# Branch B of a hybrid encoder block put in a fixed order by a list program, with branch A's norm and merge as fillers in single matmuls

## The chip, the cores and the metric

The kernel runs on one core of a Trainium2 chip. The metric is the device time of one execution in microseconds (us). Of TensorE (PE), VectorE (DVE), ScalarE (ACT), GpSimd (POOL) and SyncE (SP), PE does the matmuls and transposes, DVE and ACT the elementwise work, and POOL, SP and ACT issue transfers (DMA).

## The reference

One encoder block on 1024 tokens of 1024 features, in float32. What matters here is its token-mixing half, of which this is the frame:

```python
a_q, a_k, a_v, b_q, b_kv, i_q, i_k, i_w, gates = jnp.split(u @ w_in[l], offsets, axis=-1)
y_a = _diff_attention(a_q, a_k, a_v, slopes_a, lam, lam_init, a_subln_g[l])      # branch A, 4 heads, RMS norm behind
q_abs = jnp.einsum('bshe,rhe->bshr', b_q, w_uk[l])
o_lat = _sparse_indexed_attention(q_abs, c_kv, i_q, i_k, i_w, slopes_b)           # branch B, 8 heads, top-256 keys
y_b = jnp.einsum('bshr,rhe->bshe', o_lat, w_uv[l]).reshape(b, s, B_WIDTH)
g = jax.nn.sigmoid(gates).reshape(b, s, 2, d)
mixed = g[:, :, 0] * (y_a @ w_a_proj[l]) + g[:, :, 1] * (y_b @ w_b_proj[l])
x = _layer_norm(DEEPNORM_ALPHA * x + gate1 * (mixed @ w_o[l]), ln1_g[l], ln1_b[l])
```

The other half is a mixture of 16 experts; the adaLN factors (`mod`, from the condition and `ada_w`) go into both.

## The kernel before, in words

To keep float32 precision, an operand is split into a high and a low half and a product is three matmuls (`mm3`: low x high, high x low, high x high, lines 142, 145, 146). A split costs ACT a copy (L132) and DVE a subtraction (L128).

In order of time there are: the indexer's scores and top-k; branch A's attention, head by head (`a_attend`); branch B's attention (`b_attend`); the merge of B with the gates (the loop at L1111); w_o (`po`, L1194); the router and experts. `weave` (L75) runs two generators in turn by planned costs: `attentions` (L1044), the leaders, and `fillers` (L1066), which gives projections (`proj`, `pj` in the trace), gates, and at its end A's norm `a_norm` (L998) and the merge of A `merge_a` (L1025). `leads` and `follows` tie a filler's matmul to a leader some places back. Within these ties a scheduler that works while the kernel is built puts the instructions of each engine in order.

A head of B has 8 query rows of 128. `softmax_rows` (L768) computes a row's logits (plg: L774 with the keys' low halves, L775 with the high, L777 adds the mask of the selected keys), their minimum with the bias on DVE (L778) and the exponentials on ACT (L780). `transposed_pairs` (L783) transposes the two rows of a pair (ptr, L793) and splits them (pth on ACT, ptl on DVE), and the tail of `b_attend` multiplies by the values (pyb, L958 and L959) and adds the halves (yo, yb L962). After each second head `b_scale` (L981) multiplies by the reciprocal sums (rr, pbc) and splits (ybh, ybl). Heads' operands bqq, bqh, bql and the values bv are loaded by POOL (`b_load`, L920), one head ahead.

A's norm loads ya (L1014) by SP, spreads the factors (pbc, L1018), scales (L1019) and splits into yah, yal. The merge of A takes 8 chunks of w_ab, loaded by ACT's queue and split, and for each chunk and half 12 matmuls into pab (L1036), gates them on DVE (L1038) and stores to gates_d. Its matmuls come three at a time. The merge of B does the same with ybh and adds A's part; beside it the chunks of w_o are scaled by the adaLN gate row (L207) and split (woh, wol). `mod_rows` (L686) sums the adaLN weights adaw on DVE (macc, L694) between the projections.

Tiles rotate in slots (16 of L, 14 of X, 7 of P, 4 of pt and of sg, 2 of wr, wh, wl and b), PSUM in 8 banks: mm 2, lg 3, tp 2, av 1.

Of the kernel before, what the change touches and what calls it, by code (L numbers as in the profile page):

```python
# [12 lines left out]
FT = mybir.dt.float32  # L13
# [73 lines left out]
def block_kernel(ctx: ExitStack, tc, a, out):  # L87
# [680 lines left out]
    def softmax_rows(q, hh, ll, bias, L, sel=None):  # L768

        P = s4("P", "P")  # L770
        mx = tiny("mx")
        for n_, (c0, n) in enumerate(pieces(L)):
            p = bank("plg", "lg")
            leads(PE.matmul(p[:, :n], q, ll[:, c0:c0 + n], start=True, stop=False))  # L774
            PE.matmul(p[:, :n], q, hh[:, c0:c0 + n], start=False, stop=sel is None)  # L775
            if sel is not None:
                PE.matmul(p[:, :n], ident_bf, sel[:, c0:c0 + n], start=False, stop=True)  # L777
            V.tensor_tensor_reduce(P[:, c0:c0 + n], p[:, :n], bias[:, c0:c0 + n], 1.0, mx[:, 5:6] if n_ else 3.0e38,  # L778
                                   OP.add, OP.min, mx[:, 0:1] if n_ or L <= 512 else mx[:, 5:6])
        S.activation(P[:, :L], P[:, :L], AF.Exp, bias=mx[:, 0:1], scale=-1.0, accum_out=mx[:, 1:2])  # L780
        return P, mx
# [149 lines left out]
    rden = cp.tile([128, NB, 8], FT, name="rden")  # L931
    ybh, ybl = [None] * 4, [None] * 4

    def b_attend(c, s, yb):
        q, hh, ll = B.pop((c, s))
        v = bvt[c]
        hd = 2 * c + s
        bias = bias_tile(SL_B[hd])

        def rows(qb):  # L940
            L = (qb + 1) * 128
            sel = None
            if qb >= 2:
                j, o = MPACK[qb]
                sel = msk[j][:, o:o + L]
            P, m = softmax_rows(q[:, qb * 128:qb * 128 + 128], hh, ll, bias[:, 896 - 128 * qb:1024], L, sel)
            V.reciprocal(rden[:, qb, hd:hd + 1], m[:, 1:2])
            return P

        def tail(i, Ps):  # L950
            y = bank("pyb", "av", (128, 256))
            last = 2 * i + 1
            for kb, c0, n, th, tl in transposed_pairs(Ps, i):
                if kb % 2 == 0 and kb:
                    yield True
                mean_squares()
                st = v[kb // 4][:, kb % 4, s, :]
                PE.matmul(y[:, c0:c0 + n], st, tl, start=kb == 0, stop=False)  # L958
                PE.matmul(y[:, c0:c0 + n], st, th, start=False, stop=kb == last)  # L959
            tmp = sb.tile([128, 256], FT, name="yo", tag="yo", bufs=2)  # L960
            copy(tmp[s * 64:s * 64 + 64], y[64:128])
            V.tensor_tensor(yb[s * 64:s * 64 + 64, i * 256:i * 256 + 256], y[0:64], tmp[s * 64:s * 64 + 64], op=OP.add)  # L962
            yield True
            if s == 1 and i == 3:
                b_scale(c, yb)

        return pipelined(rows, tail)

    heads = [(c, s) for c in range(4) for s in range(2)]

    def b_main():
        for n, (c, s) in enumerate(heads):
            if s == 0:
                yb = s4("yb", "P")
            if n + 1 < len(heads):
                while heads[n + 1][0] not in have_bq:
                    yield 0.5
                b_load(*heads[n + 1])
            yield from b_attend(c, s, yb)

    def b_scale(c, yb):  # L981
        ybh[c], ybl[c] = s4("ybh", "L", dt=FR), s4("ybl", "L", dt=FR)
        for half in range(2):
            t = slice(half * 512, half * 512 + 512)
            p = bank("pbc", "tp")
            rr = s2("rr", "sg")
            r = rden[:, half * 4:half * 4 + 4, 2 * c:2 * c + 2].unsqueeze(3).to_broadcast([128, 4, 2, 64])
            copy(rr.rearrange("p (j s e) -> p j s e", j=4, s=2), r, V)
            for j in range(4):
                PE.transpose(p[:, j * 128:j * 128 + 128], rr[:, j * 128:j * 128 + 128], ident)  # L990
            V.tensor_tensor(yb[:, t], yb[:, t], p, op=OP.mult)
            copy(ybh[c][:, t], yb[:, t])
            sub(ybl[c][:, t], yb[:, t], ybh[c][:, t])


    yah, yal = [], []

    def a_norm():  # L998
        ms = yams
        while (3, 3) not in done:  # L1000
            yield 0.5
        V.tensor_scalar(ms[:, 1], ms[:, 0], 2.64e36, (1.0 - LAM_INIT) / 64.0, op0=OP.is_lt, op1=OP.mult)
        V.tensor_scalar(ms[:, 0], ms[:, 0], EPS, 1.0 / 4096.0, op0=OP.add, op1=OP.mult)
        S.activation(ms[:, 0], ms[:, 0], AF.Sqrt)
        V.reciprocal(ms[:, 0], ms[:, 0])
        V.tensor_tensor(ms[:, 0], ms[:, 0], ms[:, 1], op=OP.mult)
        for h in range(4):
            oh, ol = s4("yah", "L", dt=FR), s4("yal", "L", dt=FR)
            yah.append(oh)
            yal.append(ol)  # L1010
            for half in range(2):
                t = slice(half * 512, half * 512 + 512)
                y = s2("ya", "sg")
                dma(y, ya_d[h, :, t])  # L1014
                p = bank("pbc", "tp")
                for j in range(4):
                    i = h * 8 + half * 4 + j
                    PE.transpose(p[:, j * 128:j * 128 + 128], ms[:, 0, i:i + 1].to_broadcast([128, 128]), ident)  # L1018
                V.scalar_tensor_tensor(y, y, gsub, p, op0=OP.mult, op1=OP.mult)  # L1019
                copy(oh[:, t], y)  # L1020
                sub(ol[:, t], y, oh[:, t])
                yield 1.5


    def merge_a():  # L1025
        for c in range(KC):
            w = s4("wab", ("wh", "wl")[c % 2], (128, 2, 512), FR)
            wh, wl = halves(a["w_ab"][c, :, 0:512], w[:, 0], w[:, 1], V, S.dma_start)
            for half in range(2):
                t = slice(half * 512, half * 512 + 512)  # L1030
                g = s2("gate", "sg")
                dma(g, gates_d[c, :, t])
                p = bank("pab", "mm")
                for k in range(4):
                    cs = slice(k * 128, k * 128 + 128)
                    mm3(p, wh[:, cs], wl[:, cs], yah[k][:, t], yal[k][:, t], k == 0, k == 3, True)  # L1036
                    yield 2.5
                V.tensor_tensor(g, p, g, op=OP.mult)  # L1038
                dma(gates_d[c, :, t], g)

    started, have_bq = [-1], set()
    TOPK_MORE = 30.0
# [1 line left out]
    def attentions():  # L1044
        LAG[0] = 12
        yield from scores()
        yield from scaled(1.4, topk())
        yield TOPK_MORE

        hold[0] = filled[0]  # L1050
        LAG[0] = 40
        for h in range(4):
            while h not in A:
                yield 0.5
            started[0] = h
# [5 lines left out]
        LAG[0] = 40  # L1061
# [24 lines left out]
    weave(attentions(), fillers())  # L1086
    run(flush())


    def mixed(name):  # L1090
# [772 lines left out]
```

## Time and profile before

| what | value |
|---|---|
| median of 3 runs | 1381.33 us (1376.26 to 1382.92) |
| profiled execution, its own time | 1378.06 us |
| its span, first to last instruction | 1376.3 us |
| mean granted TensorE clock | 0.957 |
| PE busy | 1244.6 us (90%) |
| DVE busy | 952.8 us (69%) |
| ACT busy | 671.6 us (49%) |
| POOL busy | 125.8 us (9%) |
| branch B, first logits to last values | 603.1 to 870.9 us |

Busy time of PE is the union of its matmuls' records; a record is longer than the interval to the next matmul, since they are pipelined, so the interval between starts is what one costs. In brackets behind an instruction stand the idle time before it and what ended it. A granted clock of 1.00 is 2.4 GHz, the slower level 1.2 GHz.

### The profile page before, as it was taken

To read this page: it belongs to the slowest core of one execution; us is meant where nothing else is said; L and a number is where in the kernel's file an instruction comes from. 1 tells how busy PE (TensorE), PEld (TensorE's weight loads), DVE (VectorE), ACT (ScalarE), POOL (GpSimd) and SP (SyncE) were. 2 spreads that over 40 slices of the span, in tenths; PEclk is the share of its full clock that TensorE was granted. 3 is DMA by queue.
4 is the path that set the end of the run, shared out by engine and by line. 5 is a ranking of instruction groups with operands and counts; after the bars stand their busy time and mean duration, and the time that the engine had idled before them with its cause. 6 is when DMAs were issued, how large, how long until landed. Compare 5 with 4: busy or idle time off the path is not lost. (4 is left out here: it accounts for less than half of the span.)

```text
span 1376.3 us, 18450 instructions
## 1 busy us (share of the span) xinstructions
PE 1244.6 (90%) x6184; PEld 976.1 (71%) x6199; DVE 952.8 (69%) x2065; ACT 671.6 (49%) x1193; POOL 125.8 (9%) x154
## 2 busy tenths in 40 slices
PE   7999999999999999998889998899994888999950
PEld 6876778877777777666667776787873767788830
DVE  6547689783457758664676768787887778877736
ACT  4536662213785555444746556434223556555405
POOL 1000000000000001001001100000002233333120
PEclk9999999999999999998999999999996999999975
DMA  9211442113124317564545531665535798989856
GB/s 363 83 44 70 146 176 85 47 67 121 52 83 145 130 55 235 179 190 124 141 138 149 149 103 54 208 220 173 204 121 203 248 317 268 309 289 305 241 88 248
DMA packets 109526, 226.18 MB, mean 164 GB/s; under 512 B 34144, under 2 KB 40688, under 8 KB 109424
## 3 DMA queue, kind: packets, MB, share of 16 engines
q1 hardware_dynamic: 68992, 164.29, 34.0%
q0 software_dynamic: 35824, 52.23, 14.2%
q10 hardware_dynamic: 4608, 8.39, 1.9%
q8 instruction: 53, 0.87, 0.3%
q14 instruction: 49, 0.40, 0.1%
HBM read 170.15 MB, written 54.64 MB: 163 GB/s over the span
## 5 line engine op out<-in xcount | busy, mean ns | idle before, releaser
L142 PE MATMUL pj<-uh,wl 128*128 128x512 f32 x544 | 221.5, 407 | 1.5 <-ACT bkr L132 0.8
L145 PE MATMUL pj<-ul,wh 128*128 128x512 f32 x544 | 217.3, 399 | 0.0
L146 PE MATMUL pj<-uh,wh 128*128 128x512 f32 x544 | 216.8, 399 | 0.0
L128 DVE TENSOR_TENSOR ewl<-raw,ewh 128x1024 fp32r<-128x1024 f32 x102 | 122.6, 1218 | 33.8 <-ACT ewh L132 32.6
L132 ACT ACTIVATE ewh<-raw 128x1024 fp32r<-128x1024 f32 x102 | 105.8, 1057 | 61.7 <-DMA raw<-w_exp 58.5
L142 PEld LDWEIGHTS pj<-uh,wl 128*128 128x128 f32 x544 | 103.1, 189 | 35.2 <-issue 11.1
L146 PEld LDWEIGHTS pj<-uh,wh 128*128 128x128 f32 x544 | 102.9, 189 | 26.3 <-issue 5.6
L145 PEld LDWEIGHTS pj<-ul,wh 128*128 128x128 f32 x544 | 103.2, 190 | 23.8 <-issue 5.1
L132 ACT ACTIVATE pth<-ptr 128x512 fp32r<-128x512 f32 (+1 forms) x120 | 65.7, 551 | 70.2 <-PE ptr L793 38.9
L128 DVE TENSOR_TENSOR ptl<-ptr,pth 128x512 fp32r<-128x512 f32 (+1 forms) x120 | 75.3, 633 | 24.8 <-ACT pth L132 24.3
L142 PE MATMUL pgu<-ewh,xl 128*128 128x512 f32 x200 | 80.7, 404 | 0.9 <-DVE xl L128 0.6
L793 PE MATMUL ptr<-ident,P 128*128 128x128 f32 x432 | 72.5, 284 | 9.4 <-DVE ptl L128 7.9
L146 PE MATMUL pgu<-ewh,xh 128*128 128x512 f32 x200 | 79.0, 395 | 0.0
L145 PE MATMUL pgu<-ewl,xh 128*128 128x512 f32 x200 | 78.9, 394 | 0.0
L765 ACT ACTIVATE P<-P,mx 128x128 f32<-128x128 f32 (+7 forms) x64 | 49.4, 772 | 41.4 <-DVE mx L762 38.1
L793 PEld LDWEIGHTS ptr<-ident,P 128*128 128x128 f32 x432 | 51.9, 146 | 17.6 <-DVE ptl L128 8.2
L1631 POOL DMA_INDIRECT acc_d<-ot,idxs x24 | 46.7, 1946 | 188.4 <-DVE ot L1630 113.7
L128 DVE TENSOR_TENSOR wl<-raw,wh 128x512 fp32r<-128x512 f32 x68 | 44.8, 685 | 23.2 <-ACT wh L132 22.8
L780 ACT ACTIVATE P<-P,mx 128x128 f32<-128x128 f32 (+3 forms) x64 | 49.4, 772 | 22.8 <-DVE mx L778 21.6
L758 PE MATMUL plg<-ak,aq 64*128 64x512 f32 (+4 forms) x288 | 58.2, 375 | 0.9 <-DVE mx L762 0.9
L444 DVE SCALAR_TENSOR_TENSOR sc<-relu,iw,sc 128x512 f32<-128x512 f32 (+3 forms) x70 | 45.4, 654 | 18.2 <-ACT relu L439 16.3
L142 PE MATMUL po<-woh,mxl 128*128 128x512 f32 x128 | 52.5, 410 | 3.2 <-DVE r L1213 3.0
(440 smaller groups left out, 2893.7 us busy)
## 6 DMA issues: line engine op xcount, KB each, us to landing
raw<-w_exp SPq DMA_DIRECT2D x102, 512.0 KB, 8.3
raw<-w_main SPq DMA_DIRECT2D x68, 256.0 KB, 3.2
adaw<-ada_b SPq DMA_DIRECT2D x32, 512.0 KB, 4.7
adaw<-ada_a SPq DMA_DIRECT2D x16, 512.0 KB, 10.1
gates_d<-gt SPq DMA_DIRECT2D x32, 256.0 KB, 2.0
gate<-gates_d SPq DMA_DIRECT2D x32, 256.0 KB, 4.0
xt<-xT SPq DMA_DIRECT2D x8, 512.0 KB, 9.2
bv_d<-bvs SPq DMA_DIRECT2D x16, 256.0 KB, 2.9
```

Source lines behind the costliest of these rows:

```text
L128: e.tensor_tensor(o, i0, i1, op=OP.subtract)
L132: return S.activation(o, i, AF.Copy)
L142: i = PE.matmul(o, wl, xh, start=first, stop=False)
L145: PE.matmul(o, wh, xl, start=False, stop=False)
L146: e = PE.matmul(o, wh, xh, start=False, stop=last)
L444: V.scalar_tensor_tensor(acc, r[:, :n], w, acc, op0=OP.mult, op1=OP.add)
L758: i = PE.matmul(p[:, :n], q[a_][r, qs], k[b_][r, c0:c0 + n], start=m == 0, stop=m == 2)
L765: S.activation(P[:, :L], P[:, :L], AF.Exp, bias=mx_[:, 0:1], scale=-1.0, accum_out=mx_[:, 1:2])
L780: S.activation(P[:, :L], P[:, :L], AF.Exp, bias=mx[:, 0:1], scale=-1.0, accum_out=mx[:, 1:2])
L793: leads(PE.transpose(p[:, c:c + 128], Ps[s][:, kb * 128:kb * 128 + 128], ident))
L1631: G.indirect_dma_start(out=acc_d, out_offset=bass.IndirectOffsetOnAxis(ap=isc, axis=0), in_=ot, in_offset=None, compute_op=OP.add)
```

## The change

`b_attend`, `b_main`, `b_scale`, `a_norm` and `merge_a` give way to `b_stage`. It describes every step of the 8 heads, of A's norm and of A's merge as a node: an engine, a planned duration, a priority, the nodes it depends on, and the slots and banks it takes and gives back. A loop then repeatedly takes the node that can start earliest by this plan (ties by priority: heads by their number, fillers 1000, A's factors and gating -1) and writes its instructions; for PE, DVE and ACT the written order is the order of execution. It runs after the weave, so all projections and A's attention stand ahead of it. The merge of A is 192 nodes of one matmul each. The loads of w_ab go from ACT's queue to SP's, yb from a slot of P to one of wl, rr from sg to wr, and A's pbc from the bank tp to mm.

```diff
+    def b_stage():
+        HOP = 0.35
+        nodes, tokens = [], {"lg": 3, "tp": 2, "av": 1, "mm": 2, "P": 7, "pt": 4, "wl": 2, "wh": 2, "sg": 4, "b": 2, "wr": 2}
...
+                    lg = node("PE", (3 if sel else 2) * 0.00045 * w + 0.05, prio, [lg, prev_row], logits,
+                              take=("lg",) + (("P",) if n_ == 0 else ()))
+                    mins.append(node("DVE", 0.16 + 0.00105 * w, prio, [lg] + mins[-1:], least, give=(("lg", lg),)))
...
+                e = node("ACT", 0.42 + 0.00095 * L, prio, mins, exp)
...
+                    tr = node("PE", 0.00095 * w, prio, [rows_[0][1], rows_[1][1], prev_turn], turn, take=("tp",),
+                              give=[("P", x[0]["owner"]) for x in rows_] if end else ())
+                    hi = node("ACT", 0.1 + 0.001 * w, prio, [tr, prev_high], high, take=("pt", "pt"))
+                    lo = node("DVE", 0.1 + 0.00115 * w, prio, [hi], low, give=(("tp", tr),))
+                    prev = node("PE", 0.00095 * w, prio, [lo, prev], values, take=("av",) if b0 == 0 else (),
+                                give=(("pt", hi), ("pt", hi)))
...
+                ld = node("ACT", 0.0, FILL, [prev], lambda x=x: fetch_ya(x), take=("sg",))
+                ld["lag"] = 3.0
+                f = node("PE", 0.46, FILL, [ld, before_f], turn, take=("mm",))
+                d = node("DVE", 0.76, -1, [f], factor, give=(("mm", f),))
...
+            raw = s2("raw", "wr")
+            dma(raw, a["w_ab"][c, :, 0:512])
...
+            ld["lag"] = 4.0
...
+                ld = node("ACT", 0.0, FILL, [normed[-1], prev], fetch_gate, take=("sg",))
+                ld["lag"] = 3.0
...
+                        x = node("PE", 0.23, FILL, [x, wl_, normed[2 * k + half], before_f], mm, take=("mm",) if k + m == 0 else (),
+                                 give=(("wh", of_w),) if half and k + m == 5 else ())
...
+                node("DVE", 0.69, -1, [x], gated, give=(("mm", mm0), ("sg", ld)))
...
+        with tc.manual_schedule(engines={ET.PE, ET.DVE, ET.Activation}):
+            while any(left.values()):
+                best = None
+                for e, ns in left.items():
+                    for n in ns:
+                        if any(d["end"] is None for d in n["deps"]):
+                            continue
+                        at = slots(n)
+                        if at is None:
+                            continue
+                        at = max([busy[e]] + [d["end"] + (0.0 if "lag" in n else d.get("lag", 0.0)) + (HOP if d["eng"] != e else 0.02) for d in n["deps"]]
+                                 + [x + HOP for x in at if x])
+                        key = (round(at, 2), n["prio"])
+                        if best is None or key < best[0]:
+                            best = key, n, at
+                _, n, at = best
...
+                n["fn"]()
+                n["end"] = busy[n["eng"]] = at + n["dur"]
...
-        load_masks()
-        yield from scaled(1.4, b_main())
         yield from flush()
...
-        yield from a_norm()
-        yield from merge_a()
 
     weave(attentions(), fillers())
     run(flush())
+    mean_squares()
+    load_masks()
+    b_stage()
```

In the changed kernel B's logits are lines 994, 995 and 997, its transposes 1037, its values 1054 and 1055, A's merge matmuls 1198.

PE's order at the start of branch B, before (`pj` is a projection, `x4` a repeat, the mask's name carries a number):

```order
L774 MATMUL plg<-bql,bqq 128x384
L775 MATMUL plg<-bqh,bqq 128x384
L777 LDWEIGHTS ident_bf
L777 MATMUL plg<-mask_5970,ident_bf 128x384
L142 MATMUL pj<-uh,wl 128x512
L793 MATMUL ptr<-ident,P 128x128
L145 MATMUL pj<-ul,wh 128x512
L146 MATMUL pj<-uh,wh 128x512
L142 MATMUL pj<-uh,wl 128x512
```

and now:

```order
L142 MATMUL pj<-uh,wl 128x512
L145 MATMUL pj<-ul,wh 128x512
L146 MATMUL pj<-uh,wh 128x512
L994 MATMUL plg<-bql,bqq 128x128
L995 MATMUL plg<-bqh,bqq 128x128
L994 MATMUL plg<-bql,bqq 128x256
L995 MATMUL plg<-bqh,bqq 128x256
L994 MATMUL plg<-bql,bqq 128x384
L995 MATMUL plg<-bqh,bqq 128x384
L997 LDWEIGHTS ident_bf
L997 MATMUL plg<-mask_6252,ident_bf 128x384
```

All projection matmuls now stand ahead of B's first logits, which follow one another with none between them.

PE's order in the middle of the stage, before:

```order
L793 MATMUL ptr<-ident,P 128x128 x4
L142 MATMUL pab<-yah,wab 128x512
L145 MATMUL pab<-yal,wab 128x512
L146 MATMUL pab<-yah,wab 128x512
L142 MATMUL pab<-yah,wab 128x512
L145 MATMUL pab<-yal,wab 128x512
L146 MATMUL pab<-yah,wab 128x512
L142 MATMUL pab<-yah,wab 128x512
L145 MATMUL pab<-yal,wab 128x512
L146 MATMUL pab<-yah,wab 128x512
L793 MATMUL ptr<-ident,P 128x128 x4
```

and now:

```order
L1054 MATMUL pyb<-ptl,bv 128x128
L1055 MATMUL pyb<-pth,bv 128x128
L1037 MATMUL ptr<-ident,P 128x128 x4
L1198 MATMUL pab<-yah,wab 128x512 x2
L1037 MATMUL ptr<-ident,P 128x128 x4
L1198 MATMUL pab<-yal,wab 128x512
L1198 MATMUL pab<-yah,wab 128x512 x2
L1054 MATMUL pyb<-ptl,bv 128x256
L1055 MATMUL pyb<-pth,bv 128x256
L1054 MATMUL pyb<-ptl,bv 128x256
L1055 MATMUL pyb<-pth,bv 128x256
L1198 MATMUL pab<-yal,wab 128x512
```

The merge's matmuls stood nine in a row between two groups of transposes; now one to three stand in each of several places.

ACT's order at the end of branch B, before:

```order
L780 ACTIVATE P,mx<-P,mx 128x896
L780 ACTIVATE P,mx<-P,mx 128x1024
L132 ACTIVATE woh<-raw 128x512 x2
L132 ACTIVATE pth<-ptr 128x384
L132 ACTIVATE yo<-pyb 64x256
L217 DMA raw<-w_o 128x512 x2
L132 ACTIVATE pth<-ptr 128x512
L132 ACTIVATE yo<-pyb 64x256
L132 ACTIVATE pth<-ptr 128x512
L132 ACTIVATE woh<-raw 128x512 x2
L132 ACTIVATE pth<-ptr 128x384
```

and now:

```order
L132 ACTIVATE yo<-pyb 64x256
L132 ACTIVATE pth<-ptr 128x512 x2
L132 ACTIVATE pth<-ptr 128x384
L132 ACTIVATE yo<-pyb 64x256
L217 DMA raw<-w_ab 128x512
L217 DMA raw<-w_o 128x512
L132 ACTIVATE ybh<-yb 128x512 x2
L132 ACTIVATE wab<-raw 128x512
L217 DMA raw<-w_o 128x512
L132 ACTIVATE woh<-raw 128x512
```

The loads of w_o and the high halves woh stood between B's last copies; now they, and the first load of w_ab for B's merge, come behind the last of them.

## Rows read from the trace of the kernel before

**Rows 1.** Busy us by stretch: PE, PEld, DVE, ACT, POOL, then clock, DMA share, GB/s.

```profile
420.00:600.00 180.00, 179.12 (x915) 131.81 (x913) 129.53 (x322) 97.34 (x195) 6.12 (x10) 1.00 0.48 156
600.00:878.00 278.00, 246.19 (x1366) 194.31 (x1381) 185.06 (x484) 153.78 (x309) 18.69 (x31) 0.94 0.45 132
...
620.00:640.00 20.00, 15.62 (x81) 13.66 (x82) 7.80 (x15) 5.51 (x11) 2.76 (x4) 0.83 0.41 124
740.00:760.00 20.00, 19.55 (x119) 15.93 (x120) 14.43 (x44) 13.26 (x28) 2.09 (x4) 1.00 0.55 143
```

**Rows 2.** Timeline of PE, 741 to 755 us: start, duration, instruction, repeats.

```profile
741.88 0.40 PE L142 MATMUL pab<-yah,wab 128*128 128x512 f32 x1
742.11 0.39 PE L145 MATMUL pab<-yal,wab 128*128 128x512 f32 x1
...
750.15 0.62 PE L793 MATMUL ptr<-ident,P 128*128 128x128 f32 x4
750.53 0.48 PE L142 MATMUL pab<-yah,wab 128*128 128x512 f32 x1
...
754.60 0.28 PE L958 MATMUL pyb<-ptl,bv 128*128 128x256 f32 x1
754.72 0.28 PE L959 MATMUL pyb<-pth,bv 128*128 128x256 f32 x1
```

**Rows 3.** Groups by form, 600 to 878 us: count, busy us, mean ns, idle before.

```profile
L793 PE MATMUL ptr<-ident,P 128*128 128x128 f32 x306 | 51.8, 287 | 9.4 <-DVE ptl L128 7.9 <-ACT P L780 1.1 <-DVE yb L991 0.2
L958 PE MATMUL pyb<-ptl,bv 128*128 128x256 f32 x128 | 42.6, 351 | 5.8 <-DVE ptl L128 3.2 <-DVE yb L962 1.7 <-ACT yo L132 0.5
...
L128 DVE TENSOR_TENSOR ptl<-ptr,pth 128x512 fp32r<-128x512 f32 x51 | 34.8, 687 | 15.6 <-ACT pth L132 15.5
...
L142 PE MATMUL pab<-yah,wab 128*128 128x512 f32 x64 | 28.9, 451 | 0.3 <-ACT yah L132 0.3
...
L774 PE MATMUL plg<-bql,bqq 128*128 128x512 f32 x40 | 19.3, 482 | 4.5 <-DVE mx L778 4.5
L142 PE MATMUL pj<-uh,wl 128*128 128x512 f32 x43 | 19.1, 445 | 0.0
```

**Rows 4.** Waits, 600 to 878 us: total us, times, longest.

```profile
POOL bql L263 <- PE plg L775: 88.3, 5, 24.2
...
ACT pth L132 <- PE pyb L958: 25.0, 13, 4.3
ACT P L780 <- DVE mx L778: 21.6, 25, 2.5
...
DVE macc L694 <- DMA adaw<-ada_b: 11.4, 5, 4.5
```

**Rows 5.** Timeline of PE and of DVE at the stall near 620 us.

```profile
623.57 0.58 PE L145 MATMUL py<-ptl,avh 128*128 128x256 f32 x1 [4.83 <-DVE ptl L128]
...
618.25 1.29 DVE L694 SCALAR_TENSOR_TENSOR macc<-adaw,cond,macc 128x1024 f32<-128x1024 f32 x1 [4.47 <-DMA adaw<-ada_b]
```

**Rows 6.** Chain of waits near the end of branch B.

```profile
848.90 4.44 DMA row<-mod_d
853.37 0.70 DVE raw L207
```

**Rows 7.** Timeline of POOL, one issue of a head's loads.

```profile
749.06 0.78 POOL L263 DMA_DIRECT2D bql<-bk  x1 [18.27 <-PE plg L775]
```

**Rows 8.** DMA issues, 560 to 880 us: count, KB each, median us to landing.

```profile
gate<-gates_d SPq DMA_DIRECT2D x21, 256.0 KB, 5.4
adaw<-ada_b SPq DMA_DIRECT2D x8, 512.0 KB, 7.9
...
bqh<-bk POOLq DMA_DIRECT2D x7, 512.0 KB, 17.3
...
raw<-w_ab ACTq DMA_DIRECT2D x13, 256.0 KB, 3.5
...
ya<-ya_d SPq DMA_DIRECT2D x8, 256.0 KB, 5.3
```

More of the change, by code (lines that the diff above doesn't have):

```diff
@@ L932, in block_kernel @@
     ybh, ybl = [None] * 4, [None] * 4
[L934 to L967, printed above, removed]
@@ L969, in block_kernel @@
-    heads = [(c, s) for c in range(4) for s in range(2)]
-    def b_main():
-        for n, (c, s) in enumerate(heads):
-            if s == 0:
[L974 to L993, printed above, removed]
@@ L996, in block_kernel @@
-    yah, yal = [], []
-    def a_norm():
-        ms = yams
[L1000 to L1006, printed above, removed]
+    heads = [(c, s) for c in range(4) for s in range(2)]
@@ L1012, in a_norm @@
                 t = slice(half * 512, half * 512 + 512)
[L1013 to L1021, printed above, removed]
@@ L1022, in a_norm, with turn @@
-                yield 1.5
-    def merge_a():
-        for c in range(KC):
-            w = s4("wab", ("wh", "wl")[c % 2], (128, 2, 512), FR)
-            wh, wl = halves(a["w_ab"][c, :, 0:512], w[:, 0], w[:, 1], V, S.dma_start)
+                z = {}
+                x = 2 * h + half
+                def turn(h=h, half=half, z=z):
+                    z["p"] = bank("pbc", "mm")
+                    for j in range(4):
+                        i = h * 8 + half * 4 + j
+                        PE.transpose(z["p"][:, j * 128:j * 128 + 128], ms[:, 0, i:i + 1].to_broadcast([128, 128]), ident)
@@ new lines, in factor @@
+                def factor(z=z, x=x):
+                    z["y"] = ya_.pop(x)
+                    V.scalar_tensor_tensor(z["y"], z["y"], gsub, z["p"], op0=OP.mult, op1=OP.mult)
+                ld = node("ACT", 0.0, FILL, [prev], lambda x=x: fetch_ya(x), take=("sg",))
+                prev = ld
+                ld["lag"] = 3.0
+                f = node("PE", 0.46, FILL, [ld, before_f], turn, take=("mm",))
+                before_f = f
+                d = node("DVE", 0.76, -1, [f], factor, give=(("mm", f),))
@@ new lines, in b_stage, with weights_a @@
+                e = node("ACT", 0.64, FILL, [d], lambda z=z, t=t, oh=oh: copy(oh[:, t], z["y"]))
+                normed.append(node("DVE", 0.69, FILL, [e], lambda z=z, t=t, oh=oh, ol=ol: sub(ol[:, t], z["y"], oh[:, t]),
+                                   give=(("sg", ld),)))
+        ws = {}
+        def weights_a(c):
+            w = s4("wab", "wh", (128, 2, 512), FR)
+            raw = s2("raw", "wr")
+            dma(raw, a["w_ab"][c, :, 0:512])
+            ws[c] = [w[:, 0], w[:, 1], raw]
@@ L1029, in merge_a @@
+        prev = prevw = None
+        for c in range(KC):
+            ld = node("ACT", 0.0, FILL, [prevw], lambda c=c: weights_a(c), take=("wh", "wr"))
+            ld["lag"] = 4.0
+            wh_ = node("ACT", 0.64, FILL, [ld], lambda c=c: copy(ws[c][0], ws[c][2]))
+            wl_ = node("DVE", 0.69, FILL, [wh_], lambda c=c: sub(ws[c][1], ws[c][2], ws[c][0]), give=(("wr", ld),))
+            of_w = ld
+            prevw = ld
             for half in range(2):
                 t = slice(half * 512, half * 512 + 512)
-                g = s2("gate", "sg")
@@ L1032, in merge_a, with fetch_gate @@
-                dma(g, gates_d[c, :, t])
-                p = bank("pab", "mm")
+                z = {}
+                def fetch_gate(c=c, t=t, z=z):
+                    z["g"] = s2("gate", "sg")
+                    dma(z["g"], gates_d[c, :, t])
+                ld = node("ACT", 0.0, FILL, [normed[-1], prev], fetch_gate, take=("sg",))
+                prev = ld
+                ld["lag"] = 3.0
+                x = ld
                 for k in range(4):
                     cs = slice(k * 128, k * 128 + 128)
-                    mm3(p, wh[:, cs], wl[:, cs], yah[k][:, t], yal[k][:, t], k == 0, k == 3, True)
-                    yield 2.5
@@ L1038, in merge_a, with mm @@
-                V.tensor_tensor(g, p, g, op=OP.mult)
-                dma(gates_d[c, :, t], g)
+                    for m in range(3):
+                        def mm(k=k, m=m, cs=cs, c=c, t=t, z=z):
+                            if k + m == 0:
+                                z["p"] = bank("pab", "mm")
+                            w, y = ((ws[c][1], yah[k]), (ws[c][0], yal[k]), (ws[c][0], yah[k]))[m]
+                            PE.matmul(z["p"], w[:, cs], y[:, t], start=k + m == 0, stop=k == 3 and m == 2)
+                        x = node("PE", 0.23, FILL, [x, wl_, normed[2 * k + half], before_f], mm, take=("mm",) if k + m == 0 else (),
+                                 give=(("wh", of_w),) if half and k + m == 5 else ())
+                        if k + m == 0:
+                            mm0 = x
+                        before_f = x
@@ new lines, in gated, with slots @@
+                def gated(c=c, t=t, z=z):
+                    V.tensor_tensor(z["g"], z["p"], z["g"], op=OP.mult)
+                    dma(gates_d[c, :, t], z["g"])
+                node("DVE", 0.69, -1, [x], gated, give=(("mm", mm0), ("sg", ld)))
+        busy = {"PE": 0.0, "DVE": 0.0, "ACT": 0.0}
+        left = {e: [n for n in nodes if n["eng"] == e] for e in busy}
+        def slots(n):
+            at, turn = [], dict(turns)
+            for k in n["take"]:
+                at.append(free[k][turn[k]])
+                turn[k] = (turn[k] + 1) % len(free[k])
+            return None if None in at else at
@@ new lines, in b_stage @@
+        with tc.manual_schedule(engines={ET.PE, ET.DVE, ET.Activation}):
[14 more added lines that the diff above has]
+                _, n, at = best
+                left[n["eng"]].remove(n)
+                for k in n["take"]:
+                    n["got"].append((k, turns[k]))
+                    free[k][turns[k]] = None
+                    turns[k] = (turns[k] + 1) % len(free[k])
+                n["fn"]()
+                n["end"] = busy[n["eng"]] = at + n["dur"]
+                for k, owner in n["give"]:
+                    x = next(x for x in owner["got"] if x[0] == k)
+                    owner["got"].remove(x)
+                    free[k][x[1]] = n["end"]
```

146 lines of the change are left out of this document (145 added, 1 removed).

## The prediction

> **What bounds the kernel now.** I read the busy times by stretch first. In the 180 us before branch B, TensorE (PE) is busy 179.12 us at a granted clock of 1.00; from 600 to 878 us, where branch B runs, it is busy 246.19 of 278.00 us at 0.94, and VectorE (DVE), the next engine, 185.06 [rows 1]. So PE is the engine of this stretch, but it isn't full. Busy time hides most of the loss, since a matmul's record is longer than the interval to the next. So I took true prices from the timeline where PE runs without a gap [rows 2]: a 512-column matmul every 0.23 us (741.88 to 742.11), a 256-column one every 0.12 (754.60 to 754.72), four transposes in 0.38 (750.15 to 750.53).
>
> Priced so, PE's work in branch B with its fillers is:
> - logits: a head has 4,608 columns for each half of the keys and 4,224 for the masks, 13,440 in all; the large pieces are the 40 of 512 columns [rows 3]. By columns at 0.23 per 512, with a little for the narrow pieces, 6.2 us a head, 49.4 for eight;
> - values: 128 matmuls of 256 columns in the row of the ptl half [rows 3], as many for pth, at 0.12, and 64 of 128 columns at 0.085 (estimate, between a transpose and 0.12): 36.1;
> - transposes: 306 in the row [rows 3], 18 of them branch A's: 288 x 0.095 = 27.4;
> - norm factors (pbc): 64 x 0.095 = 6.1;
> - merge of A: 3 x 64 matmuls [rows 3] x 0.23 = 44.2.
>
> Sum **163 us**. After 600 us there are also 39 us of branch A's tail and projections (129 projection matmuls [rows 3] x 0.23 = 29.7, values of A 4.8, the rest small) and, before 878, 37 matmuls of B's merge, 8.5 us. Together 210 of 278 us: **about 67 us of PE's time is lost** here. That is the purse the change can draw on. It is a density of 0.76 over the stage, 0.90 in the best stretch (720 to 760: 36.1 us of priced work in 40) and 0.71 in a poor one (660 to 700: 28.5 in 40).
>
> Where does it go? The wait list [rows 4] names many short waits, none of them large: ACT's copies of transposes behind PE 25.0 us, ACT's exponentials behind DVE's minimum 21.6, DVE's adaLN sums behind their load 11.4. They are the links of one chain per query row: logits, minimum, exponential, transpose, high half, low half, values. With an in-order PE, what stands behind a link that is late is late too, filler or not. The one large stall is 4.83 us before the PE instruction at 623.57, behind DVE, which itself waited 4.47 us for an adaLN weight load [rows 5]. The granted clock is 0.83 in the slice that holds the end of that stall, 1.00 in the full slice from 740 [rows 1].
>
> **The change part by part.**
> *Projections first.* All 142 projection matmuls that before lie between B's first logits now stand ahead of them. They are 39 us of work without B's chain, and the stretch up to 600 shows that such work runs at full density [rows 1]. I add 4 us for the adaLN stall, which stays in A's tail. B's first logits move from 603 to 600 + 39 + 4 = **643 us**. That is no gain or loss by itself; what it costs is cover in B's first heads.
>
> *First heads without merge matmuls.* The first merge matmul stands after some 2.2 heads, since it needs the normed A values. Until there PE has 37.5 us of work. Per head PE, DVE and ACT each have some 14 us: by the instructions of one head at their mean durations (the largest group of DVE's, the low halves, has 0.69 us each [rows 3]) DVE has 14.5 and ACT 13.9, so nothing covers the chain. I take a density nearer the poor row, 0.76 (0.71 to 0.90): 49 us, a loss of 12, and 2 more for the start of the chain: **14**.
>
> *Then single merge matmuls.* Before, they come in threes, sixes and nines of 0.7 to 2.1 us where the weave put them; now one or two stand in each place where the list expects PE to be free. PE has 126 us left there. At the best density of before, 0.90, the loss is 14; at 0.95, 7. The new order fits the gaps better than the one that gave 0.90, so I take 0.915: **11**. The stage is 163 + 14 + 11 = **188 us**, ending at 831. DVE's work in it, 144 us, and ACT's 126, counted in the same way, fit in.
>
> *w_ab loads move from ACT's queue to SP's, yb, rr and pbc to other buffers.* ACT is rid of eight issues, off the path: nothing. SP has stores between these loads, which wait for DVE; what that can cost is in the second rival. pbc now takes one of the two banks of the merge, which has no merge to serve at that time: nothing.
>
> *What is no longer done under B.* Before, six halves of w_o were scaled and split by 878; each takes a scaling of 0.70 us [rows 6] and about as long for the low half on DVE, so 8.3 us of DVE work, and the first loads for B's merge. Now they come behind B's last row, beside B's merge, where DVE has gating, splits and w_o to do and isn't much freer than PE. Bounds: 0 if hidden, 8.3 + a landing of 3.5 for w_ab [rows 8]. I take **6**. This also removes a wait of before: at 853.37 DVE had waited for the gate row behind 4.44 us of load [rows 6].
>
> *The other queues.* POOL issues three loads of 512 KB for a head when the logits of two heads before end, as at 749.06, after 18.27 us of waiting [rows 7]. The last of them, bqh, is issued 1.6 us behind the first and lands after 17.3 us (median) [rows 8]; a head now takes 188/8 = 23.5. So they stay hidden, with some 4.6 us to spare.
>
> **Sum.** B ends at 831; with the 8.5 us of B's merge that before had done by 878 the same point is reached at 839.5, and with the 6 at 845.5: 32.5 us earlier. The profiled execution took 1378.06, so 1345.6. The median of the three runs is 3.3 above it; I say **1346.5**. What follows (w_o, router, experts) is unchanged. The bounds of the densities (a loss of 11, with 0.90 and then 0.95, to 51, with 0.76 throughout, instead of 25) alone give 1332.5 to 1372.5; those of the debt add 6 below and above.
>
> **The rivals.** A measurement can tell about 0.5%, 7 us, from no change.
>
> *Head loads bind (slower than the forecast, still faster).* A load of 512 KB issued by POOL lands in 17.3 us, one of the same size by SP (adaw) in 7.9 [rows 8]. If the difference comes from DVE, with POOL's transfers being served only in its idle time, it grows as that shrinks, from 33% before [rows 1] to 23% (144 of 188 busy): 17.3 x 33/23 = 24.8, with issue 26.4 us a head against 23.5. Six heads wait so: 17 us, 1363.5. Against it: nobody on PE waits for bql, bqq or bqh in the list; POOL waits for PE, 88.3 us [rows 4]. The Trainium skill, page "SBUF — State Buffer", section "SBUF: two separate sides", has a rule of this kind, which speaks against filling DVE: a transfer that GpSimd issues stalls while VectorE holds the port they share in some of its modes, because the descriptors can't be written meanwhile. By that rule the time is this rival's, by the rows alone the forecast's. The trace agrees so far as the two landings differ; three loads sharing one queue would explain them as well, and no row here tells which.
>
> *The loads are late and the fixed order waits (the slower side).* The list plans 3.0 us for a load of ya or of a gate and 4.0 for one of w_ab. Before they took, at the median, 5.3 us for ya, 5.4 for a gate and 3.5 for w_ab [rows 8]. The factor and gate nodes of DVE have a priority above all others, so if the list places one just when it thinks the load landed, DVE stands there, and behind it the minima, low halves and so PE. A gate's load is asked for a dozen matmuls ahead of its use; the 8 of ya and the 8 of w_ab decide. At the medians it is 8 x 2.3 for ya and nothing for w_ab: 18 us, 1364.5, still faster. SP's stores, which wait for DVE ahead of some of these loads, make them later. The change is slower from 35 us on (1381.33 - 1346.5), 2.2 us at each of the 16; if each landed only as adaw's do, after 7.9 [rows 8], it would be 8 x 4.9 + 8 x 3.9 = 70: **1416.5**. For it: the plan doesn't react. Against: 4 of the buffers of ya and the gates, and 2 of w_ab, let loads run ahead.
>
> *The chain stays the bound (no change).* If the list's durations and its 0.35 us between engines are too small, every link is late as now and the density stays at 0.76: the stage takes 163/0.76 = 214, 26 more: 1372.5, or 1378.5 with the debt at its upper bound, which I take here, since B's merge then waits for links as well. For it: each wait of [rows 4] is a few us in length, and a fixed order can't react. Against: rows of two heads overlap more and fillers are finer.
>
> *Better.* Density 0.95 throughout: loss 9 instead of 25, no debt: 1324.5.
>
> **How the numbers follow.** Forecast 0.54, head loads 0.12, better 0.13, no change 0.10, late loads 0.11. Range 1322 to 1372: it holds the first three and leaves out no change and the late loads, 0.21, but for some at its edge. Faster by over 0.5% (below 1374): forecast, head loads, better, and a little of the chain: 0.80; same 0.09; slower 0.11.
>
> **What would show it.** Right: B's first logits near 640, its last values near 830 instead of 871, PE's granted clock at 1.00 between 700 and 830, POOL's wait for logits still in the list, single merge matmuls between transposes with no gap before them. Head loads: PE's weight load at a head's first logits waits for a DMA. Late loads: DVE waits for ya or gate, or ACT for raw, by tens of us in sum. Chain: waits of the same pairs and sums as [rows 4]. Wrong altogether would be a gain or a loss that lies before 600 or behind the merge of B.

## The result, and the profile after

| what | before | after |
|---|---|---|
| median | 1381.33 us (5 runs, 1376.26 to 1383.97) | 1366.07 us (5 runs, 1362.08 to 1368.33) |
| ratio, 95% interval | | 0.9889 (0.9860 to 0.9917) |
| profiled execution, its span | 1378.06, 1376.3 | 1362.08, 1360.3 |
| branch B's first logits to its last values | 603.1 to 871.0 | 641.0 to 826.4 |
| last matmul of A's merge | 830.8 | 832.0 |
| last po matmul | 1027.6 | 1011.1 |

The change made the kernel 15.3 us faster by the medians, 16.0 by the spans of the profiled executions; 35 had been forecast. Branch B's stage did nearly what was forecast. More than half of its gain was lost again right behind it.

Busy time by stretch in the changed kernel (columns as in rows 1):

```profile
640.00:660.00 20.00, 12.67 (x69) 8.75 (x69) 9.63 (x31) 11.07 (x21) 0.07 (x1) 0.87 0.44 122
660.00:680.00 20.00, 15.15 (x100) 12.18 (x101) 16.39 (x50) 14.39 (x32) 2.35 (x3) 0.96 0.48 125
680.00:700.00 20.00, 18.39 (x128) 14.93 (x128) 19.60 (x59) 15.39 (x34) 3.10 (x6) 1.00 0.51 138
700.00:720.00 20.00, 19.93 (x127) 16.60 (x129) 17.19 (x51) 14.42 (x32) 3.12 (x5) 1.00 0.69 163
...
740.00:760.00 20.00, 19.86 (x130) 16.83 (x131) 17.43 (x51) 14.66 (x32) 3.29 (x5) 1.00 0.70 168
...
800.00:820.00 20.00, 20.00 (x133) 17.02 (x134) 15.84 (x44) 12.78 (x26) 0.00 (x0) 1.00 0.27 91
820.00:840.00 20.00, 16.07 (x81) 13.33 (x81) 11.22 (x19) 4.87 (x9) 0.00 (x0) 0.89 0.55 180
840.00:860.00 20.00, 10.12 (x33) 7.50 (x32) 11.80 (x19) 6.26 (x10) 0.00 (x0) 0.77 0.48 164
860.00:880.00 20.00, 20.00 (x90) 16.54 (x89) 15.42 (x25) 6.64 (x11) 0.00 (x0) 1.00 0.61 200
```

The first 60 us of the stage, 641 to 700, are poor, as expected of heads without cover. From 700 to 820 PE is busy 19.86 to 20.00 of 20 us at a granted clock of 1.00, where the kernel before had 15.29 to 19.55. Then, at 832, just where branch B is done, PE falls to 16.07 and 10.12 of 20 and its clock to 0.77. Before, the two slices from 840 had 16.15 and 16.40:

```profile
700.00:720.00 20.00, 15.29 (x70) 11.49 (x71) 14.66 (x34) 8.77 (x17) 0.80 (x1) 0.83 0.49 150
...
840.00:860.00 20.00, 16.15 (x98) 12.58 (x98) 15.99 (x45) 12.71 (x27) 0.00 (x0) 0.96 0.24 79
860.00:880.00 20.00, 16.40 (x82) 13.25 (x82) 15.28 (x27) 8.93 (x17) 0.00 (x0) 0.87 0.51 170
```

The changed kernel's wait list, 600 to 870 us (total, times, longest):

```profile
POOL bql L263 <- PE plg L995: 50.6, 5, 23.4
...
PE pab L142 <- DVE wab L128: 12.4, 2, 8.5
...
ACT wab L132 <- DMA raw<-w_ab: 9.1, 5, 3.3
DVE ya L1150 <- DMA ya<-ya_d: 8.9, 4, 5.8
```

POOL still waits for PE's logits before it may load a head, so the heads' loads are early. DVE waited 8.9 us for ya. New is the line of PE: it stands 12.4 us in two pieces for the low half of w_ab, the weights of B's merge. They are these on PE's timeline:

```profile
832.01 0.39 PE L1198 MATMUL pab<-yah,wab 128*128 128x512 f32 x1
836.32 0.80 PE L142 MATMUL pab<-ybh,wab 128*128 128x512 f32 x1 [3.92 <-DVE wab L128]
836.92 0.63 PE L145 MATMUL pab<-ybl,wab 128*128 128x512 f32 x1
837.34 0.63 PE L146 MATMUL pab<-ybh,wab 128*128 128x512 f32 x1
...
844.49 0.39 PE L146 MATMUL pab<-ybh,wab 128*128 128x512 f32 x1
846.26 0.50 PE L142 MATMUL po<-woh,mxl 128*128 128x512 f32 x1 [1.38 <-DVE mxl L128]
...
847.53 0.40 PE L146 MATMUL po<-woh,mxh 128*128 128x512 f32 x1
856.42 0.79 PE L142 MATMUL pab<-ybh,wab 128*128 128x512 f32 x1 [8.49 <-DVE wab L128]
```

From 832.0 nothing of branch B or of A's merge is left. PE waits 3.92 us for chunk 0 of w_ab, runs its 24 matmuls and six of po, and waits 8.49 us for chunk 1. ACT's timeline says why chunk 1 is late:

```profile
829.49 0.42 ACTq L217 DMA_DIRECT2D raw<-w_ab  x1
830.08 0.35 ACTq L217 DMA_DIRECT2D raw<-w_o  x1
...
834.91 0.63 ACT L132 ACTIVATE wab<-raw 128x512 fp32r<-128x512 f32 x1 [3.28 <-DMA raw<-w_ab]
836.30 0.36 ACTq L217 DMA_DIRECT2D raw<-w_o  x1
...
838.38 0.33 ACTq L217 DMA_DIRECT2D raw<-w_o  x1
...
843.17 0.33 ACTq L217 DMA_DIRECT2D raw<-w_o  x1
...
846.84 0.33 ACTq L217 DMA_DIRECT2D raw<-w_o  x1
...
849.43 0.34 ACTq L217 DMA_DIRECT2D raw<-w_o  x1
...
852.45 0.33 ACTq L217 DMA_DIRECT2D raw<-w_ab  x1
...
855.01 0.63 ACT L132 ACTIVATE wab<-raw 128x512 fp32r<-128x512 f32 x1 [0.73 <-DMA raw<-w_ab]
```

The raw halves rotate through two buffers (wr). Chunk 0 of w_ab takes one, and then six halves of w_o follow, in the program's order, ahead of chunk 1 (its load 852.45, its copy 855.01). Each half holds a buffer for its load, a scaling on DVE, a copy on ACT and a subtraction on DVE; six took from 830.08 to 852.45. ACT issues these loads in order, behind copies that wait for DVE. In the kernel before, two halves of w_o were loaded at 764.7 and 781.5 and lay in both buffers until the gate row came at 853 [rows 6]. Then six halves went through, their low halves between 855.1 and 870, while PE still had branch B's last rows and chunk 0 of its merge to do:

```profile
L217 ACTq DMA_DIRECT2D raw<-w_o x16: 334/334/335, 764.7 to 929.5; - x16
L128 DVE TENSOR_TENSOR wol<-raw,woh x16: 680/684/694, 855.1 to 934.5; 128x512 fp32r<-128x512 f32 x16
```

From the first scaling to the end of the last low half it takes 16.7 us there (853.4 to 870.1) and 18.8 in the changed kernel (836.2 to 855.0). The passage is about as long in both; what is new is that PE soon has nothing else to do meanwhile.

### The profile page after: what moved, and what is told of

It is laid out like the page before. It is cut to its first block, busy times and chain, and to the rows that moved or that the text cites. A ratio compares the mean times of both kernels' runs of the same rounds, so it can differ in the third digit from the quotient of the medians.

```text
span 1360.3 us, 18426 instructions
## 1 busy us (share of the span) xinstructions
PE 1228.1 (90%) x6184; PEld 969.7 (71%) x6199; DVE 950.2 (70%) x2065; ACT 665.4 (49%) x1189; POOL 128.1 (9%) x154
## 4 chain that ended last, share of the span: by engine, by line
PE 42%; DMA 20%; DVE 9%; issue 5%; ACT 2%; SPq 0%; POOLq 0%; another core or an unknown queue 0%; DVEq 0%; POOL 0%; ACTq 0%
DMA acc_d<-ot,idxs 7%; PE pj L142 4%; PE pj L146 4%; PE pj L145 4%; PE pab L1198 3%; PE plg L758 3%; DMA adaw<-ada_b 3%; PE ptr L1037 2%; PE po L142 2%; PE po L146 2%; PE po L145 2%; DMA raw<-w_o 2%; PE pgu L146 1%; PE pgu L142 1%; PE pgu L145 1%
## 5 line engine op out<-in xcount | busy, mean ns | idle before, releaser
L145 PE MATMUL po<-wol,mxh 128*128 128x512 f32 x128 | 51.3, 401 | 0.2 <-DVE wol L128 0.2
L146 PE MATMUL po<-woh,mxh 128*128 128x512 f32 x128 | 50.9, 401 | 0.0
```

The lines of the kernel that those rows point to most:

```text
L145: PE.matmul(o, wh, xl, start=False, stop=False)
L146: e = PE.matmul(o, wh, xh, start=False, stop=last)
```

## The experiments

Executions of the same code differ: B's first logits lie at 641.0 in the changed kernel's profile, at 638.0 to 647.9 in nine kernels whose code is the same up to there. So the reading goes by two intervals within each profile: the **stage**, from B's first logits to the last matmul of branch B and of A's merge, and the **seam**, from there to the start of the last po matmul. Where the code of the stage is the same (after, seam, no_scale and raw_pt), it lies between 191.0 and 193.0.

| kernel | median us | ratio to before (interval) | stage | seam | last low half of w_o begins after the stage's end |
|---|---|---|---|---|---|
| before | 1381.33 | | (with projections) 267.9 | 156.6 | 63.5 |
| after | 1366.07 | 0.9889 (0.9860 to 0.9917) | 191.0 | 179.1 | 82.8 |
| threes | 1374.91 | 0.9922 (0.9890 to 0.9954) | 196.2 | 179.1 | 83.9 |
| proj_first | 1380.56 | 0.9987 (0.9964 to 1.0009) | 229.2 | 157.2 | 65.5 |
| seam | 1366.90 | 0.9871 (0.9836 to 0.9906) | 193.0 | 170.7 | 78.5 |
| seam_before | 1394.73 | 1.0075 (1.0045 to 1.0105) | 260.9 | 161.0 | 68.8 |
| wab_in_list | 1365.67 | 0.9887 (0.9850 to 0.9923) | 189.6 | 174.4 | 80.6 |
| wab_pool | 1367.49 | 0.9905 (0.9871 to 0.9940) | 190.4 | 175.5 | 83.8 |
| no_scale | 1476.84 | 1.0724 (1.0633 to 1.0814) | 191.6 | 176.9 | 76.2 |
| norm_first | 1366.84 | 0.9901 (0.9861 to 0.9942) | 194.3 | 176.8 | 83.3 |
| raw_pt | 1355.80 | 0.9779 (0.9708 to 0.9850) | 192.5 | 164.3 | 72.0 |
| raw_pt_list | 1360.43 | 0.9819 (0.9754 to 0.9884) | 192.9 | 165.3 | 73.2 |
| raw_pt_sp | 1360.21 | 0.9826 (0.9762 to 0.9890) | 190.4 | 167.5 | 69.8 |
| raw_pt_before | 1388.48 | 1.0018 (0.9981 to 1.0055) | 264.2 | 163.8 | 70.3 |

**What made the stage short: proj_first and threes.** The first is the kernel before with B held back until all projections are given:

```diff
+        while not projected:
+            yield 0.5
         load_masks()
         yield from scaled(1.4, b_main())
```

> The kernel before with one thing added: branch B starts only when all projections have been given, so that, as in the changed kernel, its fillers are A's norm and merge alone; the order is still the weave's. If the list's order makes the stage dense, B starts near 641 here too but runs at 0.71 to 0.80 and its last values come at 845 to 870; the time is 1370 to 1385. If putting the projections ahead does it, the last values come near 830 and the time is 1360 to 1368.

It starts B at 638.8 and ends its values at 868.0, near where the kernel before did (871.0):

```profile
L959 PE MATMUL pyb<-pth,bv x160: 272/281/415, 650.1 to 868.0; 128*128 128x256 f32 x128, 128*128 128x128 f32 x32
```

So putting the projections ahead gains nothing by itself: the stage takes 229.2 us, 163 us of work at 0.71 (0.73 with the 18 matmuls of B's merge, 4.1 us, that run before its last values). The time is that of before, within its interval, and the first case of the expectation held. The list's order, with single matmuls, takes 191.0.

The second makes a node of three matmuls again:

```diff
-                    for m in range(3):
-                        def mm(k=k, m=m, cs=cs, c=c, t=t, z=z):
+                    def mm(k=k, cs=cs, c=c, t=t, z=z):
+                        for m in range(3):
...
-                        x = node("PE", 0.23, FILL, [x, wl_, normed[2 * k + half], before_f], mm, take=("mm",) if k + m == 0 else (),
+                    x = node("PE", 0.69, FILL, [x, wl_, normed[2 * k + half], before_f], mm, take=("mm",) if k == 0 else (),
```

> The changed kernel with the merge of A as 64 nodes of three matmuls (0.69 us) instead of 192 of one. If the single matmuls carry the density of 0.94 that the stage has from 700 us on, it falls back toward 0.90 and the stage is 5 to 10 us longer; if the list's order alone carries it, the stage ends within 2 us of 832 and the time within 4 us of 1366.

The stage is 196.2 us, at the lower edge of the first case; the time, 1374.91, is beyond the second's. So of the 38 us between 229.2 and 191.0, the single matmuls carry 3 to 5, the matmuls of B's merge in proj_first 4, and the list's order the rest. All else of the change is in that rest as well (the buffers that moved, SP for w_ab, w_o's six halves that no longer run beside B); it was not taken apart further.

**The poor start: norm_first.** A's norm goes ahead of the heads, so that the merge can cover them sooner.

```diff
-        FILL = 1000
+        FILL, NORM = 1000, -2
...
-                f = node("PE", 0.46, FILL, [ld, before_f], turn, take=("mm",))
+                f = node("PE", 0.46, NORM, [ld, before_f], turn, take=("mm",))
```

> The changed kernel with A's norm ahead of the heads in the list (priority -2 instead of 1000), so that A's merge can cover the first heads sooner: its first matmul stands 132 rows earlier on PE. In the changed kernel the first 59 us of the stage held 37.3 us of priced PE work. If PE lacks cover there, the stage, 191.4 us, gets 5 to 12 us shorter; if VectorE bounds that part (19.6 of 20 us busy from 680 to 700), or the late loads of ya do, it gets less than 3 us shorter or longer.

By the prediction's prices, the first 58 us now hold 41.9 us of work instead of 37.3 in 59, but the merge's matmuls run out sooner (825.4 the last, values to 836.1), and the stage is 194.3. Cover is only moved, and the rival's side of the expectation held; whether by VectorE or by ya's load isn't told apart.

**The seam, first by order: seam and seam_before.** The loads of B's merge come first, w_o's between its chunks:

```diff
-    wab = [load_wab(0)]
-    load_wo(range(3))
+    wab = [load_wab(0), load_wab(1)]
...
+        if c + 2 < KC:
+            wab.append(load_wab(c + 2))
+        if c in (1, 3, 5):
+            load_wo([c // 2])
```

> The changed kernel with another order of loads behind branch B: the first two chunks of w_ab for B's merge are loaded before any of w_o, and w_o's first three chunks after B's merge chunks 1, 3 and 5 instead of six halves ahead of chunk 1. Theory (queue for the two raw buffers): in the changed kernel PE stood 8.49 us for the low half of chunk 1 because its raw buffer came free only after six halves of w_o. Then this stall goes, the 3.92 us before chunk 0 stays, B's merge ends 8 to 11 us sooner than at 897 and the time falls by 7 to 12 us, to 1354 to 1359. Rival (VectorE's work behind B is the bound): the w_o work only moves, PE waits for wol at the first po matmuls, the time stays within 3 us of 1366. Rival (transfers are late because the DMA engines are busy there): chunks 1 and 2 land as late as before, and the stall stays.

> The kernel before with the same order of loads. There w_o's first six halves were prepared while branch B still ran. Theory (the queue hurts only where B no longer covers it): no change, within 4 us of 1381. Rival (the new order of loads is a gain of its own): faster by 7 us or more.

The 8.49 us are gone; PE's waits in the seam are now:

```profile
PE po L142 <- ACT woh L132: 5.5, 2, 5.0
...
PE pab L142 <- DVE wab L128: 2.4, 1, 2.4
...
PE po L142 <- DVE r L1425: 2.1, 1, 2.1
```

The seam is 8.4 us shorter, but 5.5 us of waits for w_o have come at po, and the medians are equal: the 1354 to 1359 of the theory were missed, and the time is the first rival's. From the first expert matmul to the end it takes 328.7 us in this kernel and in its twin from the kernel before, against 320.8 and 320.4. The edit costs that in a part that it doesn't touch, and in the profile of the twin it is 8.3 of a loss of 8.5 us; the twin came out slower, against what was expected. All profiles show this: 320.4 to 322.5 us in the five kernels whose w_o loads are those of before and after, 324.3 to 328.7 in the eight that load w_o in another order or through other buffers (no_scale left aside). Why stays open; where an edit shortens the seam, this takes a part of the gain.

**Then by sooner loads, less work on VectorE, a shorter chain.** wab_in_list gives the first two chunks of w_ab to the list as fillers; wab_pool also moves w_o's subtraction to GpSimd; no_scale leaves w_o's scaling out.

```diff
+            ld = node("ACT", 0.0, FILL + 1, [prevb, yb_of[3]], lambda c=c: weights_b(c), take=(("wh", "wl")[c], "wr"))
+            hb = node("ACT", 0.64, FILL + 1, [ld], lambda c=c: copy(wsb[c][0], wsb[c][2]))
+            node("DVE", 0.69, FILL + 1, [hb], lambda c=c: sub(wsb[c][1], wsb[c][2], wsb[c][0]), give=(("wr", ld),))
```

```diff
-            h_, l_ = halves(a["w_o"][k], s4("woh", tag, dt=FR), s4("wol", tag, dt=FR), V, S.dma_start, times=g1r)
+            h_, l_ = halves(a["w_o"][k], s4("woh", tag, dt=FR), s4("wol", tag, dt=FR), G, S.dma_start, times=g1r)
```

```diff
-            h_, l_ = halves(a["w_o"][k], s4("woh", tag, dt=FR), s4("wol", tag, dt=FR), V, S.dma_start, times=g1r)
+            h_, l_ = halves(a["w_o"][k], s4("woh", tag, dt=FR), s4("wol", tag, dt=FR), V, S.dma_start)
```

> The changed kernel with the first two chunks of w_ab for B's merge loaded (by SP) and split as fillers of the list, and behind the stage one chunk of w_o after each of the next w_ab chunks. Theory (the seam's loss is the queue for the raw buffers and ACT's queue): PE's two waits for the low half of w_ab, 3.92 and 8.49 us in the changed kernel, go; from the last matmul of A's merge to the last po matmul it takes 163 to 168 us, where the changed kernel took 179, and the time falls by 8 to 15 us. Rival (VectorE bounds the seam: gating, splits and w_o are some 62 us there, against 44 of PE's merge): the waits move to po for the halves of w_o, the interval stays above 172, the time within 5 us of 1366.

> The same with the low halves of w_o computed by GpSimd instead of VectorE (16 subtractions, 11 us of VectorE's time). If VectorE bounds the seam, the interval from the stage's end to the last po matmul is 5 us or more below that of the kernel without this; if the loads do, it is the same within 3 us, or longer where GpSimd's subtraction is slow and PE waits for wol.

> The changed kernel without the scaling of w_o by the adaLN gate row: 16 instructions of 0.69 us on VectorE are left out. The scaling stands in the raw buffers' chain (load, scaling, copy, subtraction). If that chain is the seam's loss, the wait before chunk 1 falls from 8.49 by 3 to 5 us and the interval from the stage's end to the last po matmul, 179 us, by as much. If VectorE's work is it, by 8 to 11 us. If the loads' own time is it, by less than 2.

With wab_in_list PE starts B's merge at 832.9, 0.2 us after the stage, and its waits for w_ab are 3.3 us instead of 12.4:

```profile
PE pab L142 <- DVE wab L128: 3.3, 2, 1.9
PE po L142 <- ACT woh L132: 3.0, 1, 3.0
```

Yet the seam is only 4.7 us shorter: a wait of 3.0 for woh and slower spacing take their place. Seam and time lie where the rival, VectorE as the bound, had put them; the next two runs test it. The last low half of w_o comes 80.6 us after the stage's end, as in after, 82.8. Eleven us of VectorE's work less (wab_pool) leave the seam at 175.5. GpSimd's subtraction took 1.60 us, VectorE's 0.69, so each buffer was also held longer, and this run alone doesn't clear VectorE. Without the scaling the seam is 176.9, 2.2 less than after's, and the wait before chunk 1 falls by as much, from 8.49 to 6.3; that lies between two cases of the expectation and far below the 8 to 11 us that VectorE's work as the bound would give. So VectorE's work alone isn't the bound. (The time of no_scale says nothing: the router gets other values, and the expert stage alone takes 434 us.) The theory that chunk 1 stands badly in the queue was too small: whatever goes first, 24 halves pass through two buffers.

**The buffers: raw_pt, and three with it.** w_o's raw halves go to the four buffers pt, which only the gates of A's part use by then:

```diff
-            h_, l_ = halves(a["w_o"][k], s4("woh", tag, dt=FR), s4("wol", tag, dt=FR), V, S.dma_start, times=g1r)
+            h_, l_ = halves(a["w_o"][k], s4("woh", tag, dt=FR), s4("wol", tag, dt=FR), V, S.dma_start, tag="pt", times=g1r)
```

> The changed kernel with the raw halves of w_o in the four buffers that the gates of A's part use (pt), so that the two raw buffers of wr serve w_ab alone. In the changed kernel 24 halves went through the two buffers one after the other: the last low half of w_o began 82.8 us after the end of the stage, 78.5 and 80.6 in two other orders of loads. Theory (two raw buffers, each taken for load, scaling, copy and subtraction, bound the seam): that falls to 60 to 72 us, PE's waits before w_ab go, and from the end of the stage to the last po matmul it takes 160 to 170 us instead of 179. Rival (VectorE's 62 us of work with its links, in a fixed order, bounds it): the last low half still begins 76 us or more after the stage's end, the interval stays above 173.

> Both: w_o's raw halves in pt, and the first two w_ab chunks of B's merge as fillers of the list. If buffers and queue add up, the interval from the stage's end to the last po matmul is 158 to 166 us and the time 1346 to 1356; if VectorE bounds the seam it is above 171 and the time within 5 us of 1366.

> The kernel before with w_o's raw halves in pt. There the last low half of w_o began 63.5 us after the last values of branch B, since six halves had been prepared ahead. If two raw buffers are what binds only where branch B no longer covers w_o, the time stays within 4 us of 1382; if they bind there too, it falls by 5 to 10 us.

> As the second of these, with the loads of w_ab and w_o issued by SP instead of ACT. On ACT's queue a load stands behind copies that wait for VectorE (ACT stood 6.80 us for the last scaling, 2 to 3 us at many others). If that order on ACT holds the loads back, the interval gets 3 us or more shorter than with ACT's queue; if SP's own stores and gate loads stand in the way, longer; if neither, the same within 3 us.

raw_pt's waits of PE in the seam, and its last low half of w_o (first and last start at the end of the numbers):

```profile
PE pab L142 <- DVE wab L128: 3.5, 1, 3.5
...
PE po L145 <- DVE wol L128: 2.4, 1, 2.4
...
L128 DVE TENSOR_TENSOR wol<-raw,woh x16: 682/684/693, 836.7 to 909.7; 128x512 fp32r<-128x512 f32 x16
```

The seam falls from 179.1 to 164.3 us and the last low half of w_o comes 72.0 us after the stage, both within what was expected, though 3.5 us of wait stay before chunk 0. The median is **1355.80 us**: faster than both kernels, with an interval that lies just below that of the change. The edit does two things, more buffers for w_o and two for w_ab alone; which of them carries the gain was not told apart.

The same edit to the kernel before leaves its time where it was by the interval (1.0018; the median is 6.5 us above 1382, outside the 4 us expected). But it isn't the plain control that its expectation took it for. Branch B's own halves pth and ptl use pt, and w_o's first load and first low half come only as B ends:

```profile
L217 ACTq DMA_DIRECT2D raw<-w_o x16: 334/334/368, 871.5 to 938.0; - x16
...
L128 DVE TENSOR_TENSOR wol<-raw,woh x16: 683/687/695, 878.8 to 942.5; 128x512 fp32r<-128x512 f32 x16
```

So there w_o lost its cover, as by the change, and its seam, 163.8, is that of raw_pt. Read together, losing the cover makes the seam 22.5 us longer with two buffers (156.6 to 179.1) and 7 to 8 with six (to 163.8 and 164.3). Some of this is work that was done ahead: before its stage's end the kernel before has run 18 matmuls of B's merge (4.1 us), raw_pt_before 27, after and raw_pt none.

With the first chunks in the list as well (raw_pt_list), the seam is 165.3, within the range but no shorter than without them, and the time, 1360.43, misses its range; so the sooner loads and the buffers don't add up. SP instead of ACT in that kernel makes 167.5, the same within 3 us, as the third case of that expectation had it.

## Why the prediction was right and wrong

*What bounds the kernel*: right. The loss of 67 us in branch B was PE's time, and an order with fewer late links got more than half of it back (28.7 us are lost in the new stage).

*B's start*: 643 forecast, 641.0 measured, where the nine others have 638.0 to 647.9. PE waited 1.3 us for A's low halves instead of 4.8.

*The stage*: 188 us forecast, 191.0 measured; its end 831 and 832.0. Its two terms were off in opposite ways. The first heads lost 21.7 us (59.0 with 37.3 of work), not 14: the forecast had counted DVE's work there (it was busy 45.6 of 59 us), but not that DVE would stand for ya and PE behind it, for 4.95 of the 7.7 us more:

```profile
656.82 0.75 DVE L1150 SCALAR_TENSOR_TENSOR ya<-ya,smalls,pbc 128x512 f32<-128x512 f32 x1 [5.79 <-DMA ya<-ya_d]
657.62 1.11 PE L1146 MATMUL pbc<-ident,yams 128*128 128x128 f32 x4 [4.95 <-DVE ya L1150]
```

The rest lost 7 (132.0 with 125.1), not 11: density 0.95, above the best stretch of before, and from 700 to 832 the list names no wait of PE.

*What is no longer done under B*: this is the term that failed. It was put at 6 us, between 0 and 11.8, from VectorE's work on six halves plus one landing. By 878 the kernel before had done 37 matmuls of B's merge. The changed kernel came to the same point at 860.7, 28.7 us after its stage, of which these matmuls are 8.5: the term was **20 us**. 13.8 of it are PE's waits (3.92, 8.49 and 1.38), 1.4 the six po matmuls that run ahead, and most of the last 5 the interval of 0.43 us instead of 0.23 behind the two long waits (836.92 to 837.34 and on), where the granted clock is 0.77 of full speed in the mean of the slice. The forecast had counted the work that lost its cover, and not the two buffers and the queue through which it must pass: with B above them, six halves passed while PE had B's last rows; without it they stand ahead of the weights that PE wants next. In raw_pt the same point comes 14.7 us after the stage instead of 28.7: 14 of the 20 us are back, and some 6 are left, the size that had been forecast. In seam and wab_in_list it comes even sooner, 12.7 and 12.3 us after the stage, but most of that is lost again at po: a seam is judged by its end.

*The sum*: by the profiles the point comes 17.1 us sooner (877.8 to 860.7), where 32.5 had been forecast: 14 us of the difference are this term, 3 the stage, and B's start gives 2 back. The stated median, 1346.5, is also 2.4 us below what the sum gives with its own 3.3 (1348.9).

*Head loads*: the rival didn't come. bqh lands after 18.1 us instead of 17.3 [rows 8] (the median of the four landings that the trace has, 16.6 to 19.7), while DVE's idle share fell from 33% to 19% (154.3 busy of 191.0); in proportion it would have been 30. The Trainium skill, page "SBUF — State Buffer", section "SBUF: two separate sides", says that VectorE in some of its modes holds off GpSimd's descriptors. Nothing of that kind shows in the trace, with 0.8 us between the landings; but no row tells whether VectorE's work in this stage runs in one of those modes, so the rule is neither borne out nor refuted here.

*Late loads*: right in kind, 8.9 us for ya in the place that was named and none for a gate, so far from the 35 that would have made the change slower. *Chain as the bound*: fallen, except with the weave's order (proj_first).

## What to carry to other kernels

When a stage is tightened, list what was done under its slack for the next stage, and for each piece the buffers and the queue through which it passes, in order; here its cost without cover was the time of that passage, 20 us, and not the 6 taken from the sum of its instructions. If a wait goes and the time doesn't, look at when the last piece of the same supply arrives: here that time stayed at 76 to 84 us after the stage through six edits of the changed kernel, and fell to 70 to 73 only with more buffers. And look at what a control does to the cover: an edit that takes a buffer from the covering stage also takes the cover.

## What was not expected of the hardware

GpSimd's subtraction of 128 x 512 took 1.60 us (1.28 to 2.25), VectorE's 0.69.
